# A two-layer convolution and state-space decoder step in fp32: one quarter's ratio taken at its evacuation, state-space inputs scaled on VectorE, and a rotated part kept in PSUM

## The chip, the cores and the metric

The kernel runs on one core of a Trainium2 chip. The metric is the device time of one execution in microseconds (us). PE is TensorE's matmul unit, DVE is VectorE, ACT is ScalarE, POOL is GpSimd, SP is the queue that issues most of the transfers. PSUM is the memory that PE writes its sums to; SBUF is the working memory.

## The reference, cut to what matters

```python
for i in range(DEPTH):                         # DEPTH = 2
    hp = rms_norm(yp, norm_mix[i])             # prompt 1 x 1024 x 1024, sample 8 x 8 x 1024
    ...
    # layer 0: Conformer convolution; layer 1: S5 diagonal state-space module
    yp = yp + dp
    yp = yp + swiglu(rms_norm(yp, norm_ffn[i]), ffn_w_gate[i], ffn_w_up[i], ffn_w_down[i])
...
def swiglu(h, w_gate, w_up, w_down):           # 1024 -> 2816 -> 1024
    return (jax.nn.silu(h @ w_gate) * (h @ w_up)) @ w_down
...
# state-space module: x = (b u) scaled; st = associative_scan(a, x); y = Re(c st) + d u
```

Prompt and sample tokens share the weights and stand together as 1088 columns (128 chunks and 8 sample rows, times 8 steps).

## The kernel before, in words

All products are fp32 made of three reduced-precision products: an operand is split into a high part (a copy on ScalarE, line 592) and a low part (a subtraction on VectorE, line 593).

The feed-forward part of a layer multiplies in the manner of Strassen and Winograd: a 2 x 2 split of features and of tokens, seven products (numbered 1 to 7) for eight. `ffn_up` runs over eleven blocks q of the inner dimension. In each it runs a unit "gate" and then a unit "up" (class `Seven`), and each unit does its products in the order 1, 2, 6, 7, 5, 4, 3. A product is 24 matmuls of 272 columns for each of seven, 168 in all, into two PSUM banks. A result is kept as four quarters "11", "12", "21", "22" (feature half, token half) of 128 x 544. Products 1, 6, 7 and 3 are evacuated to SBUF by copies on ScalarE (line 754, two of 272 columns), products 2, 5 and 4 by additions on VectorE (line 760, two of 272). Some products go on in the banks of another (product 5 in those of 6, product 3 in those of 5), so they begin when that one's evacuation is done. Quarter "12" is final after product 3 with one evacuation; the others take two or more.

A quarter of the gate is then scaled by `mixed.ratio` (`f0r`, `f1r` in the rows), passed through SiLU and scaled again (`gated`, lines 781 to 783); "11" and "21" are scaled on VectorE, "12" and "22" on GpSimd. The second factor stands for the ratio of the up unit, whose quarters are not scaled themselves; line 786 multiplies the two. Lines 822 to 829 form the combinations that the down products take and store them.

During blocks 2 to 10 of layer 0 a generator `ssm_tables` (lines 487 to 529, tiles `b`, `kr`, `dd`) prepares tables of the state-space layer on POOL, DVE (lines 504 to 506, 529) and ACT (line 510, a copy of the result of line 506) beside the feed-forward work. Layer 1 has no such work.

The state-space layer goes over eight feature blocks in the order 1, 3, 5, 7, 0, 2, 4, 6, each in two halves. `swapped` scales a block's input `su` by the norm (line 1461 on VectorE for the first, line 1464 on GpSimd for seven) two blocks ahead of its use. `states` takes two products from PSUM, `p1` and `pst` (`p` and `pq` in the rows), multiplies each by a table (lines 1516 and 1518), adds them (line 1519), scans four groups (line 1521) and turns the result back (lines 1532 and 1533); `outputs` feeds it to PE again.

The order on each engine is set by a scheduler with a model of the times, not by the order of the text alone; an engine works through its own queue in that order, and a wait at its head holds what stands behind.

Of the kernel before, what the change touches and what calls it, by code (L numbers as in the profile page):

```python
# [14 lines left out]
P = 128  # L15
# [6 lines left out]
NCOL = NB + NCK  # L22
# [12 lines left out]
GF = P // C  # L35
GU = GF // 2
# [6 lines left out]
HT, QT = NT // 2, NT // 4  # L43
# [19 lines left out]
def decoder_kernel(ctx: ExitStack, tc: tile.TileContext, A):  # L63
# [181 lines left out]
    for fb in range(NFB):  # L245
        t = big(f"x{fb}")
# [446 lines left out]
    def ffn_up(layer, name, mixed, tp, temp, extra=None):  # L693
        comb = mixed.b

        class Seven:
# [44 lines left out]
            def product(self, i):  # L741
                g = self.weights(i)
                before = TAKES[i] if self.chained or i != 4 else None
                if before is None:
                    self.ps[i] = [mm_bank(f"{self.nm}m{i}_{s}") for s in range(2)]
                else:
                    self.ps[i] = self.ps[before]
                ps = self.ps[i]
                for p in range(NKP):
                    mm = halfprod(ps, g, p * P, 512, comb[i, p], before is None and p == 0, p == NKP - 1, more=before is not None)  # L750
                into = {1: "11", 6: "21", 7: "22", 3: "12"}.get(i)
                if into is not None:
                    for t, m in self.quarters(into, ps):
                        S.activation(t, m, AF.Copy)
                add = {2: "11", 5: "22", 4: "21"}.get(i)
                if i == 7 and not self.chained:
                    add = "21"
                if add is not None:
                    for t, m in self.quarters(add, ps):
                        self.evac = V.tensor_add(t, t, m)  # L760
                if i in (2, 5, 4, 3):
                    self.complete.append({2: "11", 5: "22", 4: "21", 3: "12"}[i])
                return mm
# [9 lines left out]
        for q in range(NPR):  # L773
# [3 lines left out]
            def gated(w):  # L777
                o = (int(w[1]) - 1) * HT
                r = mixed.ratio[:, o : o + HT]
                E = V if w[1] == "1" else GP  # L780
                E.tensor_mul(c[w], c[w], r)  # L781
                S.activation(c[w], c[w], AF.Silu)  # L782
                E.tensor_mul(c[w], c[w], r)

            def product(w):
                V.tensor_mul(c[w], c[w], u[w])  # L786
# [662 lines left out]
    with tc.tile_pool(name="ssm", bufs=6) as sm:  # L1449
# [5 lines left out]
        def swapped(at):  # L1455

            fb = turn[at]
            if at == 0:
                for h in range(2):
                    x = su[fb][:, h * GU : (h + 1) * GU]  # L1460
                    V.tensor_mul(x, x, step_ps[0][:, :NCOL].unsqueeze(1).to_broadcast([P, GU, NCOL]))
                V.tensor_copy(rsu, step_ps[0][:, :NCOL])
            else:
                GP.tensor_mul(su[fb], su[fb], rsu.unsqueeze(1).to_broadcast([P, GF, NCOL]))
            st = stash[fb]
            v1 = st["v1"][:, :D].rearrange("p (g h q) -> p g h q", h=2, q=PS)
            v1s = big(f"v1s{fb}")
            v1x = v1s[:, :D].rearrange("p (g h q) -> p g h q", h=2, q=PS)
            w1 = st["w1"]
            w1s = big(f"w1s{fb}")  # L1470
            for i in range(2):
                S.activation(v1x[:, :, i], v1[:, :, 1 - i], AF.Copy)
                S.activation(w1s[i * PS : (i + 1) * PS, :D], w1[(1 - i) * PS : (2 - i) * PS, :D], AF.Copy)
            st.update(v1v=v1, v1x=v1x, w1s=w1s)
# [23 lines left out]
        def states(fb, hf):  # L1498
# [14 lines left out]
            for pr in range(2):  # L1513
# [1 line left out]
                q = slice(pr * 2, pr * 2 + 2)  # L1515
                V.tensor_mul(rotv[:, q], p1v[:, :, NB:], cosv[:, q])
                S.activation(pend[:, g0 + pr * 2 : g0 + pr * 2 + 2], p1v[:, :, :NB], AF.Copy)
            V.tensor_mul(rt[:, :512], pst, st["ts"][:, o : o + 512])
            V.tensor_add(rot[:, :512], rot[:, :512], rt[:, :512])
            for k in range(GU):  # L1520
                V.tensor_tensor_scan(
                    rtv[:, k],
# [316 lines left out]
```

## Time and profile before

| what | value |
|---|---|
| median of 3 runs | 2259.38 us (2258.12 to 2261.42) |
| the profiled execution's own time | 2261.8 us |
| its span, first to last instruction | 2260.0 us |
| TensorE busy | 2146.2 us, 95% of the span |
| VectorE busy | 1662.1 us, 74% |
| GpSimd busy | 1081.7 us, 48% |
| ScalarE busy | 827.2 us, 37% |

The span is what the rows count in; the profiled execution took 1.8 us more than its span, and 2.4 us more than the median. A row of the timeline gives the start, the time that it took, engine, line, operation, tiles, count, and in brackets how long the engine had been idle before it and what ended that. In a busy engine's row a wait inside an instruction is not idle time: the instruction is longer instead.

### The profile page before, as it was taken

The page shows a single profiled execution, that of the slowest core. Times are in us where ns is not written, and L with a number is a line of the kernel's source. Part 1 is how long each engine was busy: PE and PEld are TensorE (multiplying, and loading weights), DVE is VectorE, ACT ScalarE, POOL GpSimd, SP SyncE. Part 2 cuts the span into 40 slices and gives each one's busy share as a digit, 9 for nine tenths or more (in the row PEclk, how much of TensorE's full clock was granted, in tenths as well). Part 3 has the DMA queues.
Part 4 walks back from the last instruction along what each step waited for, and adds up shares of the span by engine and source line. Part 5 has one row for each costly group of instructions (what it writes and reads, how often), then busy time and mean ns, then how long its engine had stood idle before and what let it go on. Part 6 is the DMA issues. An engine that isn't in the chain of part 4 may idle for free.

```text
span 2260.0 us, 39851 instructions
## 1 busy us (share of the span) xinstructions
PE 2146.2 (95%) x15760; PEld 2110.1 (93%) x15760; DVE 1662.1 (74%) x2458; ACT 827.2 (37%) x1618; POOL 1081.7 (48%) x1000
## 2 busy tenths in 40 slices
PE   8998878989999999999998989998999999999997
PEld 7998877989999999999998979998999999999997
DVE  7974877687799999987575973339766666778586
ACT  4201226343333333333352542215333333343352
POOL 3367864456567767745122330126444444455133
PEclk9999998999999999999999999998999999999998
DMA  5489374412445445487295762211322322388542
GB/s 215 151 234 315 123 257 155 161 51 91 155 150 177 147 166 200 149 311 268 84 339 191 271 220 95 96 68 39 126 82 82 126 82 82 121 302 299 175 126 80
DMA packets 200731, 370.73 MB, mean 164 GB/s; under 512 B 16224, under 2 KB 91104, under 8 KB 200544
## 3 DMA queue, kind: packets, MB, share of 16 engines
q1 hardware_dynamic: 175328, 355.34, 45.1%
q10 hardware_dynamic: 25216, 12.85, 2.1%
q8 instruction: 123, 2.02, 0.4%
q14 instruction: 64, 0.52, 0.1%
HBM read 259.34 MB, written 108.79 MB: 163 GB/s over the span
## 4 chain that ended last, share of the span: by engine, by line
PE 62%; DVE 21%; DMA 5%; issue 4%; POOL 3%; ACT 2%; ACTq 1%; SPq 1%; DVEq 0%; POOLq 0%
PE f1d L600 9%; PE f0d L600 9%; PE gg L131 4%; PE gv L131 4%; PE p L131 4%; PE pv L131 3%; PE pg L131 2%; PE dw L1110 1%; DVE b L529 1%; DVE f0t L786 1%; ACTq L459 1%; DVE f0t L781 1%; PE f1gate10m L600 1%; PE f1up9m L600 1%; PE f1gate9m L600 1%
## 5 line engine op out<-in xcount | busy, mean ns | idle before, releaser
L600 PE MATMUL f0d<-f0db,f0da 128*128 128x272 f32 x1848 | 236.1, 290 | 2.7 <-DVE f0db L593 1.9
L600 PEld LDWEIGHTS f0d<-f0db,f0da 128*128 128x128 f32 x1848 | 234.1, 189 | 3.7 <-DVE f0db L593 2.4
L600 PE MATMUL f1d<-f1db,f1da 128*128 128x272 f32 x1848 | 234.6, 288 | 0.8 <-DVE f1db L593 0.4
L600 PEld LDWEIGHTS f1d<-f1db,f1da 128*128 128x128 f32 x1848 | 232.7, 188 | 1.8 <-DVE f1db L593 1.0
L593 DVE TENSOR_TENSOR f1db<-f1b,f1db 128x544 fp32r<-128x544 f32 x77 | 75.6, 988 | 39.4 <-ACT f1db L592 39.4
L593 DVE TENSOR_TENSOR f0db<-f0b,f0db 128x544 fp32r<-128x544 f32 x77 | 68.8, 901 | 44.2 <-ACT f0db L592 44.1
L1110 PE MATMUL dw<-u,tz 128*128 128x128 f32 x640 | 82.0, 291 | 18.2 <-DMA tz<-in_toep 18.2
L1110 PEld LDWEIGHTS dw<-u,tz 128*128 128x128 f32 x640 | 79.8, 206 | 19.7 <-DMA tz<-in_toep 15.4
L592 ACT ACTIVATE f0db<-f0b 128x544 fp32r<-128x544 f32 x77 | 49.9, 655 | 99.7 <-PE f0d L600 86.6
L592 ACT ACTIVATE f1db<-f1b 128x544 fp32r<-128x544 f32 x77 | 49.9, 654 | 90.5 <-PE f1d L600 88.1
L593 DVE TENSOR_TENSOR f0da<-f0a,f0da 128x512 fp32r<-128x512 f32 x77 | 72.3, 947 | 11.2 <-ACT f0da L592 10.7
L593 DVE TENSOR_TENSOR f1da<-f1a,f1da 128x512 fp32r<-128x512 f32 x77 | 73.2, 959 | 6.8 <-ACT f1da L592 6.8
L235 POOL TENSOR_TENSOR f1acc<-f1acc,f1t 128x544 f32<-128x544 f32 x10 | 13.4, 1371 | 113.4 <-ACT f1t L234 113.4
L1649 DVE SCALAR_TENSOR_TENSOR gs<-gv,cst,gs 128x408 f32<-128x408 f32 (+1 forms) x24 | 12.8, 589 | 68.9 <-PE gv L131 68.2
L235 POOL TENSOR_TENSOR f1nacc<-f1nacc,f1nsq 128x544 f32<-128x544 f32 (+1 forms) x13 | 16.6, 1285 | 93.9 <-ACT f1nsq L234 93.7
L235 POOL TENSOR_TENSOR f0nacc<-f0nacc,f0nsq 128x544 f32<-128x544 f32 (+1 forms) x13 | 15.5, 1208 | 93.0 <-ACT f0nsq L234 92.9
L782 ACT ACTIVATE f0t<-f0t 128x544 f32<-128x544 f32 x44 | 29.0, 660 | 83.6 <-DVE f0t L781 63.3
L782 ACT ACTIVATE f1t<-f1t 128x544 f32<-128x544 f32 x44 | 29.0, 659 | 78.4 <-DVE f1t L781 52.8
L529 DVE SCALAR_TENSOR_TENSOR b<-kr,cst,b 128x448 f32<-128x448 f32 (+6 forms) x112 | 54.4, 486 | 1.2
L592 ACT ACTIVATE f0da<-f0a 128x512 fp32r<-128x512 f32 x77 | 47.1, 620 | 19.6 <-DMA f0a<-in_down 9.9
L592 ACT ACTIVATE f1da<-f1a 128x512 fp32r<-128x512 f32 x77 | 47.2, 621 | 14.5 <-POOL f1a L870 7.3
L491 POOL TENSOR_TENSOR b<-b,b 128x512 f32<-128x512 f32 x32 | 50.5, 1596 | 1.2
(3087 smaller groups left out, 6506.1 us busy)
## 6 DMA issues: line engine op xcount, KB each, us to landing
f0b<-td SPq DMA_DIRECT2D x77, 272.0 KB, 6.7
f1b<-td SPq DMA_DIRECT2D x77, 272.0 KB, 4.8
tz<-in_toep SPq DMA_DIRECT2D x32, 640.0 KB, 6.7
f0a<-in_down SPq DMA_DIRECT2D x40, 512.0 KB, 7.4
f1a<-in_down SPq DMA_DIRECT2D x40, 512.0 KB, 5.6
td<-f0t SPq DMA_DIRECT2D x22, 544.0 KB, 5.8
td<-f1t SPq DMA_DIRECT2D x22, 544.0 KB, 5.2
f0gate<-in_gate SPq DMA_DIRECT2D x22, 512.0 KB, 4.6
```

What stands on the lines that cost most here:

```text
L131: PE.matmul(ps[c][:, :n], a, b[:, o : o + n], start=first and i == 0, stop=last and i == 2)
L235: self.last = E.tensor_add(acc, acc, t[:, :n])
L459: S.dma_start(ed[r, c].rearrange("j g h -> g j h"), et[r * G : (r + 1) * G, : L * P].rearrange("g (j h) -> g j h", h=P),)
L491: GP.tensor_mul(v, v, b.unsqueeze(2).to_broadcast([P, GU, 2, PS]))
L529: V.scalar_tensor_tensor(tv[:, :, s:], kv[:, :, : L - s], col(K_MJ, s), tv[:, :, s:], op0=ALU.mult, op1=ALU.add)
L592: S.activation(out[:, :n], x, AF.Copy)
L593: EL.tensor_sub(out[:, n : 2 * n], x, out[:, :n].bitcast(F32))
L600: mm = PE.matmul(ps[s - at][:, :QT], a[:, ah * an + ac : ah * an + ac + P], b[:, bo : bo + QT], start=first and i == 0, stop=last and i == ...
L781: E.tensor_mul(c[w], c[w], r)
L782: S.activation(c[w], c[w], AF.Silu)
L786: V.tensor_mul(c[w], c[w], u[w])
L1110: ln["dw"] = PE.matmul(ps[:, g * P : (g + 1) * P], tz[:, (g % 2) * NM + m].rearrange("p c i -> p (c i)"), uv[:, h * GU + g, PADC - m : PAD ...
```

## The change

Three edits. In every unit but those of block 0, product 3 is evacuated to quarter "12" by a multiplication with the ratio on VectorE, for the gate and for the up unit alike, where ScalarE copied it; `gated` then leaves both of GpSimd's multiplications of "12" out. The seven inputs `su` that GpSimd scaled are scaled by VectorE in two halves of 128 x 544. In `states` the product with the second table is written back into its PSUM bank, and the addition reads it from there.

```diff
                 into = {1: "11", 6: "21", 7: "22", 3: "12"}.get(i)
-                if into is not None:
+                if into == "12" and not self.first:
+                    for k, (t, m) in enumerate(self.quarters(into, ps)):
+                        self.evac = V.tensor_mul(t, m, mixed.ratio[:, HT + k * QT : HT + (k + 1) * QT])
+                elif into is not None:
                     for t, m in self.quarters(into, ps):
                         S.activation(t, m, AF.Copy)
...
                 E = V if w[1] == "1" else GP
-                E.tensor_mul(c[w], c[w], r)
+                ready = w == "12" and q > 0
+                if not ready:
+                    E.tensor_mul(c[w], c[w], r)
                 S.activation(c[w], c[w], AF.Silu)
-                E.tensor_mul(c[w], c[w], r)
+                if not ready:
+                    E.tensor_mul(c[w], c[w], r)
...
-                GP.tensor_mul(su[fb], su[fb], rsu.unsqueeze(1).to_broadcast([P, GF, NCOL]))
+                for h in range(2):
+                    x = su[fb][:, h * GU : (h + 1) * GU]
+                    V.tensor_mul(x, x, rsu.unsqueeze(1).to_broadcast([P, GU, NCOL]))
...
-            V.tensor_mul(rt[:, :512], pst, st["ts"][:, o : o + 512])
-            V.tensor_add(rot[:, :512], rot[:, :512], rt[:, :512])
+            V.tensor_mul(pst, pst, st["ts"][:, o : o + 512])
+            V.tensor_add(rot[:, :512], rot[:, :512], pst)
```

The change moves line numbers; line 754 of the changed kernel is the new multiplication, 786 and 789 are what lines 781 and 783 were, 763 is the addition of line 760, 1472 the scaling of `su`, 1526 and 1527 are lines 1518 and 1519. TensorE's order stays as it was up to the down product of layer 0.

First place: VectorE in layer 0, at the end of the gate unit of block 5 and the beginning of its up unit. Before:

```order
L593 TENSOR_TENSOR f0up5a_7291<-f0up_1_7190,f0up5a_7291 128x512
L781 TENSOR_TENSOR f0t_1_6913<-f0t_1_6913,f0r 128x544
L783 TENSOR_TENSOR f0t_1_6913<-f0t_1_6913,f0r 128x544
L524 TENSOR_TENSOR kr_7148<-kr_7148,dd_7153 128x64
L593 TENSOR_TENSOR f0up5a_7349<-f0up_0_7188,f0up5a_7349 128x512
L527 TENSOR_SCALAR b_8_7156<-kr_7148,cst 128x512
L529 SCALAR_TENSOR_TENSOR b_8_7156<-kr_7148,cst,b_8_7156 128x64x7
L504 TENSOR_TENSOR b_5_7181<-bc_7177,Ar 128x576
L505 TENSOR_TENSOR b_6_7182<-bc_7177,Ai 128x576
L529 SCALAR_TENSOR_TENSOR b_8_7156<-kr_7148,cst,b_8_7156 128x64x6
L506 TENSOR_TENSOR b_5_7181<-b_5_7181,b_6_7182 128x576
L593 TENSOR_TENSOR f0up5a_7380<-f0up5s,f0up5a_7380 128x512
```

And in the changed kernel at the same place:

```order
L593 TENSOR_TENSOR f0up5a_7281<-f0up_1_7180,f0up5a_7281 128x512
L786 TENSOR_TENSOR f0t_1_6905<-f0t_1_6905,f0r 128x544
L754 TENSOR_TENSOR f0t_0_6904<-f0gate5m_0_6914,f0r 128x272
L754 TENSOR_TENSOR f0t_0_6904<-f0gate5m_1_6915,f0r 128x272
L789 TENSOR_TENSOR f0t_1_6905<-f0t_1_6905,f0r 128x544
L593 TENSOR_TENSOR f0up5a_7339<-f0up_0_7178,f0up5a_7339 128x512
...
L504 TENSOR_TENSOR b_5_7171<-bc_7167,Ar 128x576
L505 TENSOR_TENSOR b_6_7172<-bc_7167,Ai 128x576
L529 SCALAR_TENSOR_TENSOR b_8_7146<-kr_7138,cst,b_8_7146 128x64x5
L593 TENSOR_TENSOR f0up5a_7370<-f0up5s,f0up5a_7370 128x512
L506 TENSOR_TENSOR b_5_7171<-b_5_7171,b_6_7172 128x576
```

The two new multiplications stand between the two scalings of quarter "21", and line 506 has moved behind the subtraction of the weights' sum `f0up5s`.

Second place: GpSimd at the end of the gate unit. Before, the end of block 5's gate and the beginning of its up unit, with the two scalings of "12" (tile `f0t_0`):

```order
L783 TENSOR_TENSOR f0t_1_6913<-f0t_1_6913,f0r 128x544
L781 TENSOR_TENSOR f0t_0_6912<-f0t_0_6912,f0r 128x544
L518 TENSOR_TENSOR dd_7418<-cst,dg 128x64
L723 TENSOR_TENSOR f0gate6s<-f0gate_1_7464,f0gate_0_7462 128x512
L783 TENSOR_TENSOR f0t_0_6912<-f0t_0_6912,f0r 128x544
L730 TENSOR_TENSOR f0gate_1_7464<-f0gate_0_7462,f0gate_1_7464 128x512
```

In the changed kernel, one block earlier in the names and otherwise the same place:

```order
L789 TENSOR_TENSOR f0t_1_6360<-f0t_1_6360,f0r 128x544
L723 TENSOR_TENSOR f0gate5s<-f0gate_1_6909,f0gate_0_6907 128x512
L518 TENSOR_TENSOR dd_6863<-cst,dg 128x64
L730 TENSOR_TENSOR f0gate_1_6909<-f0gate_0_6907,f0gate_1_6909 128x512
L487 TENSOR_TENSOR b_3_6613<-b_3_6613,cst 128x512
```

GpSimd's two instructions on "12" are gone, and the weights' sums stand directly behind the scaling of "22".

Third place: VectorE in the state-space layer, in the sixth block (feature block 2). In the changed kernel the scaling of an `su` that is used two blocks later stands between the scans:

```order
L1526 TENSOR_TENSOR pq_0_13649<-pq_0_13649,ld_ts_13446 128x512
L1527 TENSOR_TENSOR r_0_0_13713<-r_0_0_13713,pq_0_13649 128x512
L1529 SCALAR_TENSOR_TENSOR r_0_1_13714<-sk_490,r_0_0_13713 128x128 x3
L1472 TENSOR_TENSOR su_13567<-su_13567,rsu 128x544 x2
L1529 SCALAR_TENSOR_TENSOR r_0_1_13714<-sk_490,r_0_0_13713 128x128
```

Before, GpSimd did this scaling when the block's load had landed, and nothing of it stood in VectorE's queue; the four scans followed each other.

## Rows read from the trace of the kernel before

**Rows 1.** The page's first part: busy time, share of the span, instructions.
```profile
PE 2146.2 (95%) x15760; PEld 2110.1 (93%) x15760; DVE 1662.1 (74%) x2458; ACT 827.2 (37%) x1618; POOL 1081.7 (48%) x1000
```

**Rows 2.** Stretches (length, busy PE, PEld, DVE, ACT, POOL, clock): layer 0, layer 1, state-space.
```profile
725.05:772.00 46.95, 45.31 (x355) 44.35 (x354) 44.57 (x63) 16.36 (x36) 33.63 (x24) 1.00 0.48 168
...
1585.90:1628.10 42.20, 42.20 (x338) 42.20 (x338) 28.32 (x39) 15.74 (x34) 18.82 (x13) 1.00 0.28 98
...
1222.00:1345.00 123.00, 106.19 (x780) 101.69 (x779) 104.44 (x219) 58.61 (x155) 37.69 (x14) 0.94 0.76 255
```

**Rows 3.** Timeline of PE in one block of layer 0.
```profile
737.27 6.46 PE L600 MATMUL f0up5m<-f0b,f0up5a 128*128 128x272 f32 x48 [0.22 <-ACT f0u L754]
744.57 3.38 PE L600 MATMUL f0up5m<-f0b,f0up5a 128*128 128x272 f32 x24 [0.84 <-DVE f0t L760]
747.79 1.05 PE L515 MATMUL kr<-b,b 128*128 128x128 f32 x8
748.60 18.33 PE L600 MATMUL f0gate6m<-f0b,f0gate6a 128*128 128x272 f32 x144
767.50 3.37 PE L600 MATMUL f0gate6m<-f0b,f0gate6a 128*128 128x272 f32 x24 [0.58 <-DVE f0t L760]
```

**Rows 4.** Timeline of DVE in the same block.
```profile
727.59 0.72 DVE L783 TENSOR_TENSOR f0t<-f0t,f0r 128x544 f32<-128x544 f32 x1 [0.72 <-ACT f0t L782]
...
728.68 1.43 DVE L593 TENSOR_TENSOR f0up5a<-f0up,f0up5a 128x512 fp32r<-128x512 f32 x1 [0.23 <-ACT f0up5a L592]
...
732.08 1.92 DVE L505 TENSOR_TENSOR b<-bc,Ai 128x576 f32<-128x576 f32 x1
...
743.48 0.68 DVE L593 TENSOR_TENSOR f0gate6a<-f0gate6s,f0gate6a 128x512 fp32r<-128x512 f32 x1
744.08 0.78 DVE L760 TENSOR_TENSOR f0t<-f0t,f0up5m 128x272 f32<-128x272 f32 x2
```

**Rows 5.** Timelines of POOL and ACT in the same block.
```profile
728.21 1.35 POOL L781 TENSOR_TENSOR f0t<-f0t,f0r 128x544 f32<-128x544 f32 x1 [1.93 <-ACT f0t L754]
...
731.47 1.90 POOL L783 TENSOR_TENSOR f0t<-f0t,f0r 128x544 f32<-128x544 f32 x1
...
735.78 0.63 ACT L510 ACTIVATE b<-b 128x512 f32<-128x512 f32 x1 [4.43 <-DVE b L506]
```

**Rows 6.** Single lines: duration in ns, least/median/most.
```profile
L505 DVE TENSOR_TENSOR b<-bc,Ai x16: 743/1332/1923, 562.7 to 941.8; 128x576 f32<-128x576 f32 x16
...
L760 DVE TENSOR_TENSOR f0t<-f0t,f0gate6m x6: 423/423/424, 757.1 to 770.4; 128x272 f32<-128x272 f32 x6
```

**Rows 7.** Groups of the state-space layer: busy us, mean ns, idle before.
```profile
L1519 DVE TENSOR_TENSOR r<-r,r 128x512 f32<-128x512 f32 x16 | 21.2, 1327 | 0.2
...
L1464 POOL TENSOR_TENSOR su<-su,rsu 128x1088 f32<-128x1088 f32 x7 | 19.3, 2760 | 43.2 <-DMA su<-hs 30.7 <-DMA ld_v<-st_v 7.8 <-DVE r L1516 4.7
```

**Rows 8.** Single lines of that layer, as in Rows 6.
```profile
L1519 DVE TENSOR_TENSOR r<-r,r x16: 657/692/2973, 1235.5 to 1327.7; 128x512 f32<-128x512 f32 x16
...
L1518 DVE TENSOR_TENSOR r<-pq,ld_ts x16: 672/682/692, 1233.8 to 1327.0; 128x512 f32<-128x512 f32 x16
```

**Rows 9.** Timeline of DVE, POOL and SP in the state-space layer.
```profile
1229.08 1.35 DVE L1461 TENSOR_TENSOR su<-su,steps 128x544 f32<-128x544 f32 x2 [1.82 <-DMA su<-hs]
...
1291.68 0.43 SPq L1447 DMA_DIRECT2D su<-hs  x1
...
1292.92 1.50 DVE L1519 TENSOR_TENSOR r<-r,r 128x512 f32<-128x512 f32 x1
1294.45 1.37 DVE L1521 TENSOR_TENSOR_SCAN r<-sk,r 128x128 f32<-128x128 f32 x4
...
1298.58 2.49 POOL L1464 TENSOR_TENSOR su<-su,rsu 128x1088 f32<-128x1088 f32 x1 [4.71 <-DVE r L1516]
...
1298.91 2.71 DVE L1519 TENSOR_TENSOR r<-r,r 128x512 f32<-128x512 f32 x1
...
1327.68 2.80 DVE L1519 TENSOR_TENSOR r<-r,r 128x512 f32<-128x512 f32 x1
```

## Prediction

> **What bounds the kernel now.** I read the page's first part, then the busy time cut by stretches, then the timelines of one block. The page says that PE is busy for 95% of the span [rows 1], so time can come only from the few per cent in which it waits, or from a stretch where it isn't the bound. The stretches show which these are [rows 2]. A feed-forward block of layer 1 takes 42.20 us, and PE is busy for all 42.20 of them, with DVE at 28.32. A block of layer 0 takes 46.95 us, and this block repeats eight times (from 584 to 960 us, cut at the same matmul) with the same period. There PE shows 45.31 busy and DVE 44.57, since the state-space tables are made beside the products. The state-space layer takes 123 us, with PE at 106.19 and DVE at 104.44: no engine is full, and they wait for one another.
>
> How much of a layer-0 block is PE's own work? A unit without a wait takes 21.10 us (half of the 42.20), and the table matmuls behind it 0.81 (they begin at 747.79, the next product at 748.60 [rows 3]); with two of each that makes 43.82. So 46.95 - 43.82 = 3.13 us of a block are waits, some of them hidden in matmul rows that look busy. The rows with a bracket tell what PE waits for: product 3 for DVE's evacuation of product 5 (line 760), 0.84 us in the up unit and 0.58 in the gate unit, and product 5 for ScalarE's of product 6, 0.22 [rows 3]. The larger ones name DVE. DVE in turn has only 46.95 - 44.57 = 2.38 us idle in a block, so I take DVE's queue as what sets this period.
>
> Part of DVE's busy time is not work. The same instruction (line 505, 128x576, both inputs in SBUF) takes between 0.743 and 1.923 us [rows 6]. The 1.92 one stands at 732.08 and ends just behind a multiplication of POOL from 731.47 that takes 1.90 [rows 4, 5]. An addition with one input from PSUM (line 760) keeps to 0.423 to 0.424 in the same block [rows 6]. So DVE and POOL hold each other up where DVE reads two operands from SBUF.
>
> [...]
>
> **Edit 1, quarter "12", layer 0.** The new multiplication has one operand in PSUM and one in SBUF, as line 760 has, in the same shape. Two of those take 0.78 us [rows 4], and I cost the new pair at 0.77. Per block:
> - Gate pair, +0.77. The order puts it between the two scalings of "21", where DVE sits idle 0.72 waiting for SiLU [rows 4]. It fills that: +0.05.
> - Up pair: no idle time stands at its place, so +0.77.
> - ScalarE copies two pairs less. Its weight copy (line 592) stood behind them, and DVE waited 0.23 for it [rows 4]. I take that as gone: -0.23.
> - POOL loses two multiplications that took 1.35 and 1.90 us [rows 5]. What they cost DVE can be read: the subtraction of line 593 at 728.68 took 1.43, which is 0.75 over the 0.68 that the same subtraction takes unhindered at 743.48; line 505 took 1.92 - 0.74 = 1.18 too long. The rows of both overlap POOL's two [rows 4, 5]. Together 1.93 us for 3.25 us of POOL, 0.59 per us. Two unhindered multiplications are 2.70 us of POOL; at 0.59 that is 1.6 of relief, which I take. The bounds: nothing, where POOL's next instruction moves up and holds DVE as long, and the whole 2.70.
>
> The sum is 0.05 + 0.77 - 0.23 - 1.6 = -1.0 us per block, and PE has 3.13 of waits to give. Over eight blocks that is **-8.1 us**. With no relief and nothing filled it is +1.54 x 8 = +12.3. With 2.70 it is -2.1 x 8 = -17. Block 0 keeps its old form and block 1 lies before the periodic stretch: 0 for both.
>
> [...]
>
> **Edit 1, layer 1.** There DVE gets 1.54 more per block, with 42.20 - 28.32 = 13.9 idle, and PE has no wait [rows 2]. Both POOL and ScalarE get less. PE's full queue hides it: 0. If the cover were gone, it would cost at most 1.54 x 11 = 17. A bank of product 3 is free when DVE, instead of ScalarE, has read it. PE comes back to it only several products later, so that is 0 as well.
>
> **Edit 2, `su` on VectorE.** The first block's two halves already stand on DVE, and took 1.35 us together [rows 9]. Seven such pairs are 7 x 1.35 = +9.45. (In the new ones both inputs lie in SBUF, so POOL can hold them up; by the row of line 505 that is up to 1.18 for one of them.) POOL gives up 19.3 us in seven instructions [rows 7]. What these held up: the addition of line 1519 takes 0.692 in the median [rows 8] but 21.2 us in sixteen [rows 7], an excess of 21.2 - 16 x 0.69 = 10.2. Single ones took 1.50, 2.71 and 2.80 [rows 9]. The 1.50 and the 2.80 stand beside POOL's other work, not `su`, and their 0.81 + 2.11 = 2.9 stay. The other 7.3 go: -7.3. In the first block nothing is queued behind `su` on POOL any more, which I take as -0.9, half of the 1.82 that DVE waited there for the load [rows 9]. One new wait comes in. The load of the `su` for a later block is issued at 1291.68, and POOL began with it at 1298.58; DVE comes to it between scans that began at 1294.45 [rows 9]. There it would now wait with the scans and the turning back queued behind it, and PE's output products behind those. That costs between 0 and 3 us, since the load may well have landed before POOL (which waited for DVE by its bracket) took it; I take +1.
>
> **Edit 3, PSUM.** Line 1518 already reads PSUM and takes 0.682, line 1519 0.692 from SBUF, in the median [rows 8]. Writing the product back to PSUM changes nothing that these rows show: 0. But the addition then has one SBUF input, and by the rows of line 760 POOL can't hold it up. So the 1.50 and the 2.80 would come down too, for up to -2.9; I take half, -1.4, since POOL may hold up the next instruction instead.
>
> [...]
>
> State-space layer: 9.45 - 7.3 - 0.9 + 1 - 1.4 = 0.85, **+1 us**. If nothing is given back it is 9.45 + 3 = +12; if the addition escapes wholly and no wait comes, about -2.
>
> **Sum.** -8.1 + 1 = -7.1 on the profiled execution's 2261.8 (span 2260.0 and 1.8 around it) makes 2254.7. The median lies 2.4 below that execution; I take the same for the changed kernel: **2252 us**.
>
> **Rivals.** This kernel's measurement can tell about 0.2%, 4.5 us, from no change.
> - *B, the relief comes in full.* Each of POOL's dropped multiplications frees its whole 1.35 on DVE. For it: the removed ones met DVE head on, both times [rows 4, 5]. Against: 1.93 was lost, not 3.25. It gives -17 + 1 = -16: 2243.
> - *C, the gain is handed to another wait.* ScalarE's table copy (line 510) waits for DVE's line 506, 4.43 us in the trace [rows 5], and ahead of the evacuation of product 6, for whose banks PE's product 5 waits 0.22 [rows 3]. The order now puts line 506 behind one more subtraction, of 1.43 when held up [rows 4]. PE's wait there can then grow by up to 1.3 per block, which eats the 1.0. For it: the 0.22 shows that there is no slack at that place. Against: DVE comes there earlier, by the relief at line 505. It gives -8.1 + 8.1 + 1: 2260, no change.
> - *D, slower: the relief doesn't come.* POOL's queue closes up, its next instructions stand where the multiplications were, and DVE is held as long by them. POOL stays busy for some 31 of 46.95 us, so DVE rarely finds it idle. Then DVE carries +0.6 (0.05 + 0.77 - 0.23) to +1.54 per block, +4.7 to +12.3, and the state-space layer +1 or more: around 2268. It decides as soon as the relief is under 0.15 us per block: then layer 0 costs (0.59 - 0.15) x 8 = 3.5, and with the 1 it is slower by what a measurement can tell.
>
> **How the numbers follow.** My forecast gets 0.45 (its own range is 2246 to 2256), B 0.10, C 0.27, D 0.18. B stays low because it needs a loss that the rows don't show. C is the strongest rival, since the order shows the move and PE has a wait at the place. Faster by over 0.2% is A and B: 0.55. Same is C: 0.27. Slower is D: 0.18. The range takes in B at one end, A and C, and at the other only the lower edge of D (4.7 + 1 on 2259.4 is 2265): 2242 to 2266. Most of D's 0.18 lies above it, and no more than 0.02 below.
>
> **What would show it.** In the changed kernel's trace a layer-0 block should take 45.9 us, not 46.95, and PE's waits for line 763 before product 3 shrink by about 1 in sum. The new line 754 should take 0.42 each, POOL's busy time per block fall from 33.6 to about 31, and line 505 lose its 1.92 rows. B would show a period under 45, C a wait of over 1 us at product 5 with ScalarE named, D a period over 47 with lines 505 and 593 as long as before. A block of layer 1 should stay at 42.20. In the state-space layer line 1527 should show about 0.69 in sixteen of sixteen, line 1472 1.35 a pair, and the stage should end within 2 us of now; a DVE idle time ended by the load of `su` would be the new wait. What would make me wrong above all is that PE's period in layer 0 doesn't hang on DVE's queue as a whole, but on one chain through ScalarE: then the 8.1 is not there, whatever DVE saves.

## The result, and the profile after

| what | before | changed |
|---|---|---|
| median | 2262.33 us (2250.02 to 2266.24, 11 runs) | 2247.10 us (2243.33 to 2254.14, 11 runs) |
| the profiled execution's own time, its span | 2261.8, 2260.0 us | 2244.88, 2243.1 us |
| VectorE busy | 1662.1 us | 1658.1 us |
| GpSimd busy | 1081.7 us | 993.5 us |

The ratio is 0.9943, with a 95% interval of 0.9930 to 0.9956: 10 to 16 us faster. The prediction was 2252 and faster, in a range that holds the result. The gain forecast (7.1 us) is a little over half of the 12.9 that the ratio makes. The kernel before has its median here over eleven runs; the forecast started from 2259.38, the median of three.

The stages show where the time went. Below are busy times by stretch in the changed kernel (columns as in [rows 2]): the second half of a block's up unit and the gate unit behind it in layer 0 (one whole period), a block of layer 1, the feed-forward blocks 2 to 10 of layer 0 from their first matmul to the down product's first, and the stretch from the start of the state-space layer to the end of the gate products behind it.

```profile
720.25:766.57 46.32, 44.70 (x354) 44.11 (x353) 43.19 (x66) 15.40 (x32) 30.11 (x22) 1.00 0.50 171
1569.07:1611.27 42.20, 42.20 (x338) 42.20 (x337) 27.93 (x40) 15.15 (x32) 15.60 (x11) 1.00 0.29 99
563.37:971.94 408.57, 396.93 (x3131) 392.51 (x3129) 371.20 (x557) 138.92 (x288) 243.51 (x170) 1.00 0.48 167
1214.77:1509.67 294.90, 279.15 (x1815) 272.51 (x1815) 165.61 (x299) 102.84 (x222) 44.21 (x26) 0.98 0.49 167
```

The same two long stretches of the kernel before:

```profile
564.29:979.22 414.93, 401.50 (x3130) 393.83 (x3129) 377.76 (x520) 147.73 (x324) 274.37 (x188) 1.00 0.47 164
1223.95:1526.81 302.86, 284.52 (x1815) 278.07 (x1816) 165.38 (x285) 102.62 (x222) 65.07 (x33) 0.96 0.48 162
```

Layer 0 gained 6.4 us and the state-space stretch 8.0; layer 1 still takes 42.20 per block [rows 2]. What is left of the 16.9 between the two spans is 2.5 us, most of it in the down product of layer 0, which took 244.7 us before and 242.8 after; with the work of before it took between 241.4 and 244.9 in the executions below.

In layer 0, PE's timeline in an up unit and the gate unit behind it in the changed kernel shows two waits:

```profile
720.21 21.34 PE L600 MATMUL f0up5m<-f0b,f0up5a 128*128 128x272 f32 x168
...
742.21 15.31 PE L600 MATMUL f0gate6m<-f0b,f0gate6a 128*128 128x272 f32 x120
758.68 3.43 PE L600 MATMUL f0gate6m<-f0b,f0gate6a 128*128 128x272 f32 x24 [1.16 <-ACT f0t L757]
762.57 3.38 PE L600 MATMUL f0gate6m<-f0b,f0gate6a 128*128 128x272 f32 x24 [0.46 <-DVE f0t L763]
```

The up unit (720.21) now runs its 168 matmuls without a wait, where before it had 0.22 and 0.84 [rows 3]. The gate unit's wait before product 3 went from 0.58 to 0.46. But a new one stands before product 4 (matmul 120): 1.16 us for ScalarE's evacuation of product 7. ScalarE's timeline tells why it is late:

```profile
757.68 0.66 ACT L787 ACTIVATE f0t<-f0t 128x544 f32<-128x544 f32 x1 [2.03 <-DVE f0t L786]
758.25 0.66 ACT L757 ACTIVATE f0t<-f0gate6m 128x272 f32<-128x272 f32 x2
```

The evacuation (line 757) stands behind the SiLU of quarter "11", which waits 2.03 us for VectorE's scaling of that quarter. So PE's idle time in the block is what it was: 1.64 us before (0.22, 0.84 and 0.58) and 1.62 now. The 0.63 us by which this block is shorter are in PE's busy time, 45.31 [rows 2] and 44.70, where waits within a row count as busy: both lie above the 43.82 that the prediction made for a block without a wait.

In the state-space layer, the groups of VectorE in the changed kernel (columns as in [rows 7]):

```profile
L1529 DVE TENSOR_TENSOR_SCAN r<-sk,r 128x128 f32<-128x128 f32 x64 | 31.9, 558 | 0.5
...
L1540 DVE TENSOR_TENSOR r<-r,ld_tc 128x512 f32<-128x512 f32 x16 | 12.2, 760 | 0.0
...
L1527 DVE TENSOR_TENSOR r<-r,pq 128x512 f32<-128x512 f32 x16 | 10.9, 683 | 0.3
L1541 DVE TENSOR_TENSOR r<-r,ld_ts 128x512 f32<-128x512 f32 x16 | 10.9, 682 | 0.0
L1472 DVE TENSOR_TENSOR su<-su,rsu 128x544 f32<-128x544 f32 x14 | 9.5, 716 | 0.6 <-DMA su<-hs 0.6
```

and of the kernel before, beside the 21.2 us of line 1519 [rows 7]:

```profile
L1521 DVE TENSOR_TENSOR_SCAN r<-sk,r 128x128 f32<-128x128 f32 x64 | 26.6, 474 | 0.4
...
L1533 DVE TENSOR_TENSOR r<-r,ld_ts 128x512 f32<-128x512 f32 x16 | 15.5, 968 | 0.0
...
L1532 DVE TENSOR_TENSOR r<-r,ld_tc 128x512 f32<-128x512 f32 x16 | 10.4, 651 | 0.0
```

The addition fell from 21.2 to 10.9, the last step of the turning back from 15.5 to 10.9, and the scaling of `su` came in with 9.5. The scans grew by 5.3, and the first step of the turning back (line 1532, now 1540) from 10.4 to 12.2. Over these four lines VectorE spends 7.8 us less than before, and 9.5 more on `su`. Cut at the end of VectorE's last turning back, the stage looks like this, before and changed:

```profile
1223.95:1333.25 109.30, 94.05 (x700) 89.74 (x700) 98.28 (x211) 55.78 (x150) 35.17 (x13) 0.94 0.80 272
```

```profile
1214.77:1319.90 105.13, 91.66 (x696) 87.17 (x696) 99.47 (x225) 55.59 (x147) 15.15 (x6) 0.95 0.84 283
```

VectorE is busy for 1.2 us longer than before, and the stage is 4.2 us shorter: VectorE's idle time went from 11.0 to 5.7. Most of that is time in which it waited for PE's products (in total, times, longest; before, then changed):

```profile
DVE r L1518 <- PE pq L1490: 3.3, 3, 2.6
DVE r L1516 <- PE p L1487: 2.9, 3, 1.3
```

```profile
DVE r L1524 <- PE p L1495: 0.6, 1, 0.6
DVE pq L1526 <- PE pq L1498: 0.5, 2, 0.4
```

The other 3.8 us of the stretch's 8.0 lie behind this cut. The kernel before has the granted clock at half there for 10 us, which the changed kernel's execution has not:

```profile
1349.70:1360.00 10.30, 9.48 (x26) 7.98 (x27) 8.30 (x8) 6.55 (x10) 0.77 (x1) 0.50 0.53 185
```

### The profile page after: what moved, and what is told of

The parts are those of the page before. It is cut to its first block, busy times and chain, and to the rows that moved or that the text cites. A ratio compares the mean times of both kernels' runs of the same rounds, so it can differ in the third digit from the quotient of the medians.

```text
span 2243.1 us, 39882 instructions
## 1 busy us (share of the span) xinstructions
PE 2135.5 (95%) x15760; PEld 2102.7 (94%) x15760; DVE 1658.1 (74%) x2552; ACT 805.2 (36%) x1538; POOL 993.5 (44%) x953
## 4 chain that ended last, share of the span: by engine, by line
PE 69%; DVE 17%; issue 4%; DMA 4%; POOL 2%; ACT 2%; ACTq 1%; SPq 0%; DVEq 0%; POOLq 0%
PE f1d L600 10%; PE f0d L600 9%; PE gg L131 4%; PE gv L131 4%; PE p L131 4%; PE pv L131 3%; PE pg L131 2%; PE dw L1116 2%; DVE r L1529 1%; DVE b L529 1%; PE f1up4m L600 1%; PE f0up7m L600 1%; PE f1gate10m L600 1%; PE f1up9m L600 1%; PE f1gate9m L600 1%
## 5 line engine op out<-in xcount | busy, mean ns | idle before, releaser
L1657 DVE SCALAR_TENSOR_TENSOR gs<-gv,cst,gs 128x408 f32<-128x408 f32 (+1 forms) x24 | 12.8, 589 | 68.4 <-PE gv L131 68.0
L235 POOL TENSOR_TENSOR f0nacc<-f0nacc,f0nsq 128x544 f32<-128x544 f32 (+1 forms) x13 | 15.5, 1210 | 92.9 <-ACT f0nsq L234 92.8
L592 ACT ACTIVATE f0da<-f0a 128x512 fp32r<-128x512 f32 x77 | 46.9, 619 | 20.2 <-DMA f0a<-in_down 5.8
```

The lines of the kernel that those rows point to most:

```text
L235: self.last = E.tensor_add(acc, acc, t[:, :n])
L592: S.activation(out[:, :n], x, AF.Copy)
L1657: V.scalar_tensor_tensor(sg[:, o : o + n], p[:, :n], col(K_BGV, fb), sg[:, o : o + n], op0=ALU.add, op1=ALU.mult)
```

## The experiments

All times of this table are from one profiled execution each, except the ratio. The two stretches are cut as above. They are a better measure than totals here: the convolution ahead of them, which no kernel changes, ended anywhere between 457 and 467 us. They vary too: five kernels leave GpSimd's work of the state-space layer as it was (before, e1, e3, e7, e8), and their second stretch takes 302.07 to 309.45.

| kernel | layer 0, blocks 2 to 10 | state space to gate products | ratio to before (95%) |
|---|---|---|---|
| before | 414.93 | 302.86 | 1 |
| changed | 408.57 | 294.90 | 0.9943 (0.9930 to 0.9956) |
| e1 edit 1 | 406.98 | 309.45 | 0.9980 (0.9964 to 0.9996) |
| e2 edit 2 | 415.02 | 297.41 | 0.9994 (0.9978 to 1.0009) |
| e3 edit 3 | 415.27 | 302.07 | 1.0008 (0.9989 to 1.0026) |
| e4 edits 2, 3 | 415.24 | 293.44 | 0.9978 (0.9962 to 0.9993) |
| e5 before, g6l on VectorE | 415.38 | 303.56 | 1.0012 (0.9998 to 1.0025) |
| e6 changed, g6l on VectorE | 407.55 | 295.59 | 0.9945 (0.9923 to 0.9967) |
| e7 edit 1's price | 420.38 | 304.68 | one run, 2260.98 us |
| e8 edit 1's relief | 402.72 | 303.80 | one run, 2251.31 us |
| e9 changed again | 406.97 | 296.75 | 0.9938 (0.9920 to 0.9957) |
| e10 SiLU behind evacuation | 415.38 | 297.69 | 0.9951 (0.9935 to 0.9967) |
| e11 all low parts on VectorE | 407.93 | 297.87 | 0.9954 (0.9939 to 0.9970) |
| e12 e10 and e11 | 412.89 | 299.56 | 0.9970 (0.9954 to 0.9985) |

**The edits one by one.** Edit 1 alone, from the change's first two places:

```diff
+                if into == "12" and not self.first:
+                    for k, (t, m) in enumerate(self.quarters(into, ps)):
+                        self.evac = V.tensor_mul(t, m, mixed.ratio[:, HT + k * QT : HT + (k + 1) * QT])
...
+                ready = w == "12" and q > 0
```

> Edit 1 alone: quarter 12 takes the ratio at its evacuation, su stays on GpSimd, the addition stays in SBUF. Theory (the feed-forward edit gave 7 us in layer 0 by relief from GpSimd, the rest of the gain lies in the state-space edits and in the granted clock behind them): layer 0 up to its down product 7.3 us earlier than before, a block 46.3 us in place of 46.95, total 2251 to 2256. Rival (the whole gain is the feed-forward edit, the state-space layer gains only because it starts at another moment): total near 2247, with the state-space layer as short as in the changed kernel.

Layer 0 gained 8.0 us, and the state-space stretch was as long as without the edits there (longer, in this execution). So the feed-forward edit isn't the whole gain.

Edit 2 alone:

```diff
-                GP.tensor_mul(su[fb], su[fb], rsu.unsqueeze(1).to_broadcast([P, GF, NCOL]))
+                for h in range(2):
+                    x = su[fb][:, h * GU : (h + 1) * GU]
+                    V.tensor_mul(x, x, rsu.unsqueeze(1).to_broadcast([P, GU, NCOL]))
```

> Edit 2 alone: the seven su scaled on VectorE. Theory (what GpSimd's scaling held up on VectorE pays for the added work, and PE's shorter waits let the granted clock stay up behind): layer 0 as before, the state-space layer 0 to 4 us shorter, total 2256 to 2262. Rival of the prediction (VectorE is the bound there, so the added 9.45 us show): 5 or more us longer, total 2266 or more.

The stretch was 5.5 us shorter in the profiled execution, more than the theory's 0 to 4; the ratio's interval goes from 5 us less to 2 us more, which is no measurable change. The rival is out: the added 9.45 us do not show.

Edit 3 alone:

```diff
-            V.tensor_mul(rt[:, :512], pst, st["ts"][:, o : o + 512])
-            V.tensor_add(rot[:, :512], rot[:, :512], rt[:, :512])
+            V.tensor_mul(pst, pst, st["ts"][:, o : o + 512])
+            V.tensor_add(rot[:, :512], rot[:, :512], pst)
```

> Edit 3 alone: the product with the second table is written back to PSUM and the addition reads it there, su stays on GpSimd. Theory (the addition escapes GpSimd, but the next instruction with two SBUF inputs is held up instead, such as the scan): the addition at 0.69 in all sixteen, the scans longer, total within 3 us of before, 2258 to 2263. Rival (the addition's excess of 10.2 us is a loss that goes away): 6 or more us shorter, 2256 or less.

Its groups of VectorE:

```profile
L1521 DVE TENSOR_TENSOR_SCAN r<-sk,r 128x128 f32<-128x128 f32 x64 | 34.3, 596 | 0.4
...
L1532 DVE TENSOR_TENSOR r<-r,ld_tc 128x512 f32<-128x512 f32 x16 | 14.5, 906 | 0.4 <-ACT r L1529 0.4
...
L1519 DVE TENSOR_TENSOR r<-r,pq 128x512 f32<-128x512 f32 x16 | 11.0, 685 | 0.4
```

The addition takes 0.685 us in the mean and 0.689 at most in all sixteen, 10 us less in sum. The scans took 7.7 us more, the turning back's line 1532 about 4. GpSimd is as busy as before (40.14 us of the first 140, against 40.20), and what the addition no longer loses to it, other lines with two SBUF inputs lose: the edit alone gives nothing.

Both:

> Edits 2 and 3 together, without edit 1. Theory (the edits add up): total as the sum of the two alone, and 7 to 9 us below before, 2252 to 2256, with the clock up where the gate products of the next step begin. Rival (the clock there was a chance of one execution): total within 3 us of before.

The edit is the last two diffs together. The stretch is the shortest of all, and the ratio 0.9978; with edit 1's 0.9980 that makes 0.9958, a little less gain than the whole change's 0.9943 (to 0.9956), and within what their own intervals allow. The theory held in part. The total fell by 5 us (1.6 to 8.6), short of the 7 to 9 expected. It is not the sum of the two edits alone either, whose ratios make 1.0002, but the intervals allow it. What edit 3 adds to edit 2 is not shown: their ratios with and without it, 0.9978 and 0.9994, overlap, and no run has edits 1 and 2 alone.

**Where the state-space stretch is decided.** I cut it into slices of 20 us. The third slice (40 to 60 us from its start) tells the kernels apart. First the kernel before, then edits 1, 3 and 2 alone, then the changed kernel (columns as in [rows 2]):

```profile
1263.95:1283.95 20.00, 16.89 (x130) 16.02 (x129) 19.80 (x33) 9.16 (x27) 11.06 (x4) 1.00 0.95 328
```

```profile
1254.32:1274.32 20.00, 14.96 (x104) 14.12 (x103) 18.08 (x26) 7.75 (x21) 10.64 (x4) 0.91 0.86 294
```

```profile
1267.53:1287.53 20.00, 14.61 (x107) 13.15 (x106) 19.66 (x30) 7.48 (x23) 10.65 (x4) 1.00 0.91 304
```

```profile
1264.68:1284.68 20.00, 18.76 (x148) 17.83 (x147) 19.84 (x46) 11.26 (x31) 2.50 (x1) 1.00 0.91 318
```

```profile
1254.77:1274.77 20.00, 19.19 (x155) 18.54 (x154) 19.83 (x48) 11.98 (x32) 2.49 (x1) 1.00 0.80 267
```

VectorE looks equally full in the kernel before and the changed one, 19.80 and 19.83. But it gets through 33 instructions before and 48 after, and PE is busy for 16.89 and 19.19. In between stand GpSimd's 11.06 and 2.49. The timelines of GpSimd and VectorE in edit 1's kernel show the worst of it:

```profile
1269.12 2.65 POOL L1573 TENSOR_TENSOR g3l<-sy,g3h 128x1088 fp32r<-128x1088 f32 x1 [8.60 <-ACT pend L1523]
1271.73 2.60 POOL L1470 TENSOR_TENSOR su<-su,rsu 128x1088 f32<-128x1088 f32 x1
...
1255.43 2.76 DVE L1538 TENSOR_TENSOR r<-r,ld_tc 128x512 f32<-128x512 f32 x1
1258.11 2.96 DVE L1539 TENSOR_TENSOR r<-r,ld_ts 128x512 f32<-128x512 f32 x1
...
1269.06 5.86 DVE L1527 TENSOR_TENSOR_SCAN r<-sk,r 128x128 f32<-128x128 f32 x4
```

Four scans take 1.37 unhindered and took 5.86 here, as long as GpSimd's low part and scaling of `su` ran back to back; the two steps of turning back, 0.65 and 0.68 unhindered, had lost as much 13 us earlier. So VectorE loses some 4.4 us in one go, twice. PE's timeline in the same kernel shows that it waits there, for the two steps of turning back and then for a copy on ScalarE, which itself came behind the scans:

```profile
1258.24 0.50 PE L1556 MATMUL py<-r,ld_w 128*128 128x136 f32 x2 [1.62 <-DVE r L1538]
...
1261.13 0.78 PE L1557 MATMUL py<-r,w1s 128*128 128x136 f32 x2 [1.63 <-DVE r L1539]
...
1275.51 1.28 PE L1493 MATMUL p<-su,ld_v 128*128 128x136 f32 x4 [2.96 <-ACT pend L1523]
```

Over all kernels PE's busy time in this slice is 14.5 to 16.9 with `su` on GpSimd (six executions) and 18.8 to 19.4 with it on VectorE (six; e11 and e12, which change GpSimd's work further, aside).

**The granted clock.** Over the first 140 us of the stretch, the mean granted clock was 0.90 to 0.94 in the six executions with `su` on GpSimd (mean 0.925), and 0.95 to 0.96 in the changed kernel's two, e4, e6 and e10 (mean 0.954). Edit 2 alone had 0.94, and e11 0.95; e12 is an exception with 0.91. First the kernel before, then the changed one:

```profile
1223.95:1363.95 140.00, 121.66 (x837) 115.21 (x838) 113.05 (x226) 67.01 (x166) 40.20 (x15) 0.91 0.76 260
```

```profile
1214.77:1354.77 140.00, 124.25 (x885) 117.61 (x886) 116.63 (x243) 69.36 (x169) 20.32 (x8) 0.96 0.77 261
```

In edit 1's kernel the granted clock was 1.00 in the 20 us ahead of the slice 1254.32 above, and fell behind PE's waits of that slice; these two stretches read 0.51:

```profile
1261.20:1264.70 3.50, 3.50 (x14) 3.48 (x15) 3.42 (x11) 1.88 (x6) 0.00 (x0) 0.51 0.40 118
1274.80:1281.70 6.90, 6.19 (x25) 6.15 (x26) 5.83 (x16) 4.32 (x13) 0.00 (x0) 0.51 0.64 228
```

Not every wait is followed by a fall: the kernel before has PE busy for 16.89 of 20 us in its slice above, at 1.00. The difference, 0.954 less 0.925 times 140, is worth, as an estimate, up to 4 us if PE were the bound throughout. To see whether such a fall can be steered I moved one instruction off GpSimd, ahead of the first gate products, where PE waited 1.7 and 1.4 us (its weight loads 2.0 and 1.67) about the time that the clock fell:

```diff
-        def halved(fb, y):
+        def halved(fb, y, E=GP):
...
-            GP.tensor_sub(lo, y, h.bitcast(F32))
+            E.tensor_sub(lo, y, h.bitcast(F32))
...
-        yn[turn[-1]] = halved(turn[-1], y)
+        yn[turn[-1]] = halved(turn[-1], y, V)
```

> The kernel before with one instruction elsewhere: the low part of the last state-space block's result (g6l) is made by VectorE, which is idle there, and not by GpSimd. PE's order is the same. PE waits there 2.0 us for g6h and 1.67 for g6l in the kernel before, and the granted clock then falls to half from 1349.7 to 1360.0. Theory (the clock falls behind PE's waits, and the two state-space edits gained by making these shorter): the second wait shrinks to about 0.5, the low stretch behind it is 3.4 us or less or gone, and the time falls by 3 to 6 us, 2255 to 2258. Rival (the clock does not hang on these waits): only the 1.2 us of the wait, the low stretch stays at 5.1.

The wait for g6l went, and the clock stayed up at that place. The slice of the kernel before, and of this one:

```profile
1343.95:1363.95 20.00, 16.91 (x69) 14.77 (x68) 9.50 (x9) 9.44 (x13) 2.51 (x1) 0.74 0.74 271
```

```profile
1266.41:1286.41 20.00, 14.48 (x100) 13.64 (x98) 18.07 (x25) 7.47 (x21) 10.58 (x4) 0.91 0.86 291
1286.41:1306.41 20.00, 19.14 (x134) 19.10 (x135) 16.67 (x41) 9.40 (x29) 2.50 (x1) 0.83 0.61 206
...
1346.41:1366.41 20.00, 18.38 (x104) 16.36 (x103) 9.49 (x11) 8.59 (x12) 0.00 (x0) 1.00 0.73 251
```

The time did not improve (1.0012). The execution has another fall, some 70 us ahead of the moved instruction, behind PE's 14.48; e1, e7 and e8 have one there too, without the move. And in e7 and e8 the clock stayed up at the later place although PE waited there as in the kernel before (1.5 to 1.7 us for g6h and 1.4 for g6l). The slice of e8 there:

```profile
1332.74:1352.74 20.00, 16.93 (x93) 14.84 (x92) 8.81 (x8) 8.36 (x12) 2.50 (x1) 1.00 0.69 238
```

So neither that the move kept the clock up, nor that it brought the earlier fall, is shown: where the clock falls differs between executions of the same work. The same instruction in the changed kernel:

> The changed kernel with the same one instruction (g6l) on VectorE. PE's order is the same. Theory (the clock no longer falls behind these waits in the changed kernel): only the second wait's own 1.0 us, 2244 to 2247. Rival (it still falls there in most executions, and the one profiled was lucky): 3 us or more below the changed kernel.

The edit is the same three lines. 0.9945 is the changed kernel's ratio within its interval: a microsecond can't be seen.

**Price and relief of edit 1.** The multiplication at the evacuation alone (edit 1's first place, without its second), and GpSimd's scalings left out alone (its second place, without the first):

```diff
+                    for k, (t, m) in enumerate(self.quarters(into, ps)):
+                        self.evac = V.tensor_mul(t, m, mixed.ratio[:, HT + k * QT : HT + (k + 1) * QT])
```

> Leaves GpSimd's two scalings of quarter 12 in place, and multiplies at the evacuation on VectorE too (12 is then scaled twice). This is the price of edit 1 without its relief. By the prediction's bounds a block of layer 0 takes 0.6 to 1.54 us more than before, 47.5 to 48.5 us. Rival (VectorE's queue is not what sets the period): 46.95 or less.

```diff
+                ready = w == "12" and q > 0
+                if not ready:
                     E.tensor_mul(c[w], c[w], r)
```

> Leaves out GpSimd's two scalings of quarter 12 from block 1 on, with ScalarE's copies as before (12 is then not scaled). This is the relief without the price. By the prediction's 1.6 us a block of layer 0 takes 45.3 us; by 2.7 or more it would be 44.2 or less, near PE's own 43.82. Rival (GpSimd's next instructions move up and hold VectorE as long): 46.5 or more.

The relief's block, in the columns of [rows 2]:

```profile
722.20:767.50 45.30, 44.71 (x354) 44.20 (x353) 42.92 (x63) 16.28 (x37) 30.33 (x21) 1.00 0.50 175
```

It takes 45.30 us, and the prediction's relief of 1.6 made 45.3. Over the stretch it is 12.2 us, in one execution. The five executions with edit 1 and no further change in layer 0 (changed, e1, e6, e9, e11) mean 407.6, which puts the price at 407.6 - 402.7 = 4.9 us on top of the relief. Without the relief the price alone (e7) showed as 5.4 us, but some 3 of these are, as an estimate, a fallen clock, in two places of 3.5 us where it read 0.51 (at 809 and 977 us), so 2 to 5. The block of e7, by the same cut, takes 47.00 us, below the 47.5 to 48.5 expected and above the rival's 46.95: without the relief the price is smaller than on top of it.

```profile
719.60:766.60 47.00, 45.12 (x351) 44.10 (x350) 45.59 (x66) 15.29 (x32) 33.48 (x24) 1.00 0.50 168
```

**The changed kernel again, and tries to better it.**

> The changed kernel once more, for a second execution's trace and as the measure of the three runs beside it. Theory (with both state-space edits PE's granted clock falls for a shorter time there than in any of the kernels without them): low stretches between the start of the state-space layer and the first gate products behind it together under 14 us (a loss of under 7 us), a block of layer 0 between 45.9 and 46.3 us, ratio to the kernel before 0.993 to 0.996. Rival (chance): low stretches as long as before, 17 us or more.

It held: 406.97, 296.75, 0.9938; the clock over the first 140 us was 0.95, so the low stretches there came, as an estimate, to some 7 us of lost clock (140 us at 0.05 less), at the edge of what was expected. Its eight periods in layer 0 average 45.8 us, just under the 45.9 to 46.3.

The SiLU of "11" put behind the evacuation of product 7:

```diff
-                        work.finish()
+                        if i in (7, 5, 4, 3):
+                            work.finish()
...
+                with tc.issue_after(work.copied.ins) if w == "11" and q > 0 else nullcontext():
                     S.activation(c[w], c[w], AF.Silu)
```

> The changed kernel with ScalarE's SiLU of the gate's quarter 11 behind the evacuation of product 7 in its queue, from block 1 on (scaling of 11 is issued after product 7's too). In the changed kernel PE waits 0.4 to 1.3 us per gate unit for that evacuation before product 4. Theory (this wait is what ate part of the relief): it is gone, a block of layer 0 takes 45.2 to 45.7 us, 5 us less than the changed kernel. Rival (VectorE's queue is the bound, and the wait only shows its lag): the wait moves to product 3, and a block takes as long as before, 45.9 to 46.3.

The wait before product 4 is gone, and the one before product 3 has taken its place. VectorE has no idle time from 754.40 until the evacuation that this product waits for, at 771.07:

```profile
750.93 18.33 PE L600 MATMUL f0gate6m<-f0b,f0gate6a 128*128 128x272 f32 x144
771.55 0.75 PE L600 MATMUL f0gate6m<-f0b,f0gate6a 128*128 128x272 f32 x3 [2.29 <-DVE f0t L763]
...
771.07 0.77 DVE L763 TENSOR_TENSOR f0t<-f0t,f0gate6m 128x272 f32<-128x272 f32 x2
```

The stretch is 7 to 8 us longer, a block 46.9 us in the mean, more than either side expected. The rival's mechanism fits: the wait moved to product 3, behind a full VectorE queue, so the wait at product 4 only showed its lag. Why the block grew by a microsecond on top of that stays open.

All low parts of the gate's input on VectorE:

```diff
-            GP.tensor_sub(lo, y, h.bitcast(F32))
+            V.tensor_sub(lo, y, h.bitcast(F32))
```

> The changed kernel with all eight low parts of the gate's input (g0l to g7l) made by VectorE, so that GpSimd does nothing in the state-space layer. Theory (GpSimd's 17.8 us there still held VectorE up for 13.5 us, and VectorE pays 8 x 1.35 = 10.8 for the subtractions): 1 to 4 us less than the changed kernel. Rival (VectorE now waits at its queue's head for the loads that these need): 2 us or more slower than the changed kernel.

> The edits of the two runs before together. Theory (they lie in different stages and add up): as much below the changed kernel as the two together, 4 to 9 us. Rival: no better than the better one of them.

Neither helps (0.9954, 0.9970), and the second is no better than either edit alone, as its rival said. In e11 the stretch is 1 to 3 us longer although GpSimd does nothing in the first 140 us. VectorE isn't held up there any more: its scans take 21.9 us in place of 31.9. But it now waits for ScalarE to make the high parts, up to 1.7 us at a time; the rival had named loads. No version that I ran beats the changed kernel.

## Why the prediction was right, and where it was not

- **The total** lies in the range, but the way there is partly luck. Layer 0 came out by the forecast's mechanism. The state-space layer had the wrong sign, and the range reached down to 2242 only for rival B, which did not come.
- **Layer 0, -8.1 forecast, -7.3 measured** (407.6 against 414.9; the kernels with the layer 0 of before took 414.93 to 415.38). The stretch holds nine blocks; cut at the eight periods that the prediction counts it is -7.3 too. Both terms came out: relief 12.2 where 1.6 a block made 12.8, price 4.9 on top of it where 0.05 + 0.77 - 0.23 a block made 4.7 (over the eight periods 11.4 and 4.1), though e7 puts the price alone lower. The two waits before product 3 shrank by 0.96 in sum (0.84 and 0.58 to nothing and 0.46), as forecast, and the 0.22 went. Line 505 kept a row of 1.91, against the forecast, but its median fell from 1.33 to 0.80. One wait of rival C's kind came: ScalarE in front of PE. It stands at product 4, not 5, and behind a SiLU, not the table copy. In the block shown it is as long as the waits that went, yet the block is shorter, and when e10 took this link away nothing was won. That fits VectorE's queue as the bound, as the prediction said, better than a chain through ScalarE.
- **Rival B** (relief in full, 2.70 a block) and **rival D** (no relief) are out: e8 shows 12.2 in all, some 1.5 a block. What the prediction read from the rows, that GpSimd holds VectorE up where it reads two operands from SBUF, is still borne out for single instructions: with edit 3 alone the addition with one PSUM input took 0.689 us at most in all sixteen, and lines with two SBUF inputs took the delay (the scans 34.3 us for 26.6, line 1532 14.5 for 10.4).
- **Layer 1, 0 forecast:** 42.20 and 42.20.
- **State-space layer, +1 forecast, about -9 measured** (the mean of changed, e4, e9 and e10 is 295.7; of before, e1, e3, e7 and e8, with `su` on GpSimd, 304.6). This is the step that failed. Most single costs were right: `su` 9.5 for 9.45, its wait for loads 0.6 for 1, the addition 0.69 in all sixteen, the product written back to PSUM 0.691 in the mean where line 1518 took 0.683. The -0.9 for the first block did not come: VectorE waited 1.82 for that load before and 1.99 after. What GpSimd held up, 7.3 and 1.4 in the forecast, came to 7.8 by the four lines that changed, but not where it was forecast: the addition and line 1533 lost 10.3 and 4.6 less, the scans and line 1532 5.3 and 1.8 more. So in this pair of executions VectorE's busy time grew by 1.2, near the forecast. What failed is that this sum was taken for the time of the stage, though the prediction itself says that no engine is full there and they wait for one another. The waits were put at nothing beside the loads, and they gave the gain: VectorE's idle time fell by 5.3 and its waits for PE's products from 6.2 to 1.1. In edit 1's kernel, GpSimd's instructions back to back cost VectorE over 4 us at places that PE waits for. That breaking these up is what shortened the waits is argued from the slices, not shown by a run of its own.
- **The granted clock** was in no term. Over the whole stretch, in the same two groups of executions, PE's busy time for the same matmuls (1814 or 1815 in a trace) fell from 283.9 to 279.7 in the mean, and its idle time from 20.7 to 16.0. So about half of the 9 us are fewer waits, and the other half, in matmul time, fits the up to 4 us of the clock, though a busy row can hide a wait. Whether fewer waits are what kept the clock up isn't shown: e5 took one wait away and gained nothing, and in e7 and e8 the clock stayed up behind such waits.
- **Edit 3's addition from PSUM, without a price in the forecast:** none is seen. Its mean of 683 to 685 ns stands against a median of 692 with both inputs in SBUF [rows 8].

The layer-0 and state-space means together make 16.2 us; the ratio's interval is 10 to 16.

## What to carry to other kernels

When an operation moves from GpSimd to VectorE, count what GpSimd holds up on every VectorE line with two SBUF inputs, before and after, not on the line where it shows most (here the addition and line 1533 lost 10.3 and 4.6 us less, the scans and line 1532 5.3 and 1.8 more). Taking one instruction out of GpSimd's way, as with the PSUM operand, gave nothing here (1.0008), since others took the delay. Take the sum of VectorE's busy time for a stage's time only where VectorE has no idle time: where it and PE wait for each other, the waits need a term of their own (here the sum grew by 1.2 us and the stage became 4.2 shorter). Look first where two GpSimd instructions stand back to back (four scans took 5.86 us for 1.37 there), and see whether PE waits at that place. Where a stage has PE waiting, compare the granted clock before and after too, over several executions.

## What was not expected of the hardware

The same instructions gave 408.57, 407.55 and 406.97 us in layer 0's stretch (changed, e6, e9). In the state-space layer the kernel before and e8 have the same instructions, and the addition took 21.2 us in all in the one and 18.2 in the other, the scans 26.6 and 33.2 (e8's rows):

```profile
L1524 DVE TENSOR_TENSOR_SCAN r<-sk,r 128x128 f32<-128x128 f32 x64 | 33.2, 577 | 0.4
L1522 DVE TENSOR_TENSOR r<-r,r 128x512 f32<-128x512 f32 x16 | 18.2, 1140 | 0.2
```

So which instructions GpSimd holds up differs from execution to execution. So does the place where the clock falls: half (0.50) for 10 us about the first gate products in the kernel before, and not at all there in e7 and e8 (1.00 in e8's slice), with the same work there and about the same waits.
